# Even mixer of a two-layer trunk: cached sequences in four column groups, their pages fetched ahead, attention of the third pair moved ahead of two recurrences

## The chip, the core and the metric

The kernel runs on one core of a Trainium2 chip. The metric is the device time of one execution in microseconds. Engines: PE is TensorE (PEld its weight loads), DVE is VectorE, ACT is ScalarE, POOL is GpSimd, SP is SyncE, which issues most DMAs.

## What is computed

One inference step of a trunk of two layers for a prompt of 512 tokens and 8 sequences of 4 sample tokens, 544 tokens side by side, in float32. Each layer is a half feed-forward, a mixer, and another half feed-forward. The change lies in layer 0's mixer:

```
def sb_block(q, q_pos, k, v, k_pos, bias):
    z = jnp.einsum('bqhd,bshd->bhqs', q, k, preferred_element_type=jnp.float32) * (SB_HEAD_DIM ** -0.5)
    z = z + bias.astype(jnp.float32)[None, :, None, None]
    mask = k_pos[None, :] < q_pos[:, None]
    log_keep = jnp.where(mask, jax.nn.log_sigmoid(-z), 0.0)
    later = lax.cumsum(log_keep, axis=3, reverse=True) - log_keep
    w = jnp.where(mask, jnp.exp(jax.nn.log_sigmoid(z) + later), 0.0)
    return jnp.einsum('bhqs,bshd->bqhd', w.astype(v.dtype), v)

def sb_lru_mixer(u, past_k, past_v, conv_buf, h0, w_in, ...):
    proj = u @ w_in
    q, k, v, xr, xg = jnp.split(proj, ...)
...
    attn = sb_attention(q, k_all, v_all, q_pos, k_pos, sb_bias).reshape(B, T, SB_WIDTH)
    xc, new_buf = causal_conv(conv_buf, xr, conv_w, conv_b)
    h, h_last = rg_lru(xc, h0, w_a, b_a, w_i, b_i, lam)
    rec = h.astype(u.dtype) * jax.nn.gelu(xg)
    out = jnp.concatenate([attn.astype(u.dtype), rec], axis=-1) @ w_out
```

There are 8 heads of 64, so four pairs of 128 features. Each sample sequence has 256 cached keys and values (past_k, past_v), held as two pages of 128 tokens that a page table picks from a pool of pages in device memory. `rg_lru` is a gated recurrence h = a h + b along the tokens, for 512 features in four tiles of 128.

## The kernel before

The residual x lies on chip as eight tiles of 128 features by 544 tokens; beside it stand xh and xl, the high and low half of the normalised x, each eight tiles. Every linear is three matmuls per tile (`mm3`, L362 to L364): high weights by xh, high weights by xl, low weights by xh, over 256 and 288 columns. Weights are fetched by SP, ACT makes their high half wh (L323) and VectorE their low half wl (L324).

`even_mixer` (L823) walks through a string of tokens, `EVEN_ORDER` (L818):

- Q, V, L, X with a number: linears of one pair's queries and keys, of its values, of a tile of the recurrence and of its output gate.
- A: prompt attention of a pair (`prompt_attention`, L696): eight pieces of 128 to 512 columns, each a chain from PE (z, L707 to L709) over ACT and VectorE (t, mx, sh, sl) back to PE (L720 to L726), to ACT (wt) and to PE again (pv, L729).
- F, G, E, S: gate weights, gates, gelu, and the recurrence of a tile (`lru_scan`, L612, the scan itself on VectorE at L624); T writes the states out; P splits a tile's result into the halves that the output linear reads, which lie in xh[4..7] and xl[4..7].
- K0 and K1: scores of sample sequences 0 to 3 and 4 to 7 against their cached keys (`sample_scores`, L741).
- W: weights from the scores (`sample_weights`, L766). U: weights times cached values (`sample_values`, L787).
- O1 and O0: output linear over the recurrence's and the attention's tiles.

The string sets priorities; a scheduler then interleaves the instructions of each engine, and the resulting order of each engine is fixed when the kernel is built. An engine, and the DMA queue of POOL, runs its own order strictly.

In K, a sequence's two pages are each fetched by an indirect DMA that POOL issues (`page`, L733) into one of six buffers, transposed in four pieces on PE (tp, L751), copied to kt by VectorE or ACT (L753, L755), and multiplied with the queries (sc, L758): 32 stationary columns, that is one group of 32 of the 128 columns of PE, 256 long. In U, wT holds the transposed weights, and each page of values is multiplied with 32 columns of it (po, L805), 512 long; a last matmul adds the sample's own tokens (L806), os and oT (L807, L812) bring the result into feature order, and four splits write it into yh and yl. A page of values is fetched when its matmul's turn comes near.

A matmul of plain float32 runs as two passes, so 32 matmul rows of the scores are 64 records in the trace.

## Time and profile before

| | |
|---|---|
| median of 3 runs | 1924.73 us (1924.58 to 1926.36) |
| profiled execution | 1924.04 us, its span 1922.3 us |
| PE busy | 1872.1 us, 97% |
| weight loads (PEld) busy | 1792.7 us, 93% |
| VectorE busy | 1080.6 us, 56% |
| ACT busy | 836.6 us, 44% |
| POOL busy | 125.5 us, 7% |
| mean granted clock of PE | 0.993 |

The span runs from the first to the last instruction. Busy time of matmuls contains their pipelined tails, so a busy PE is not PE at its peak. The even mixer's second half, in which the change lies, is the stretch from about 470 to 600 us.

### The profile page before, as it was taken

How to read it: one execution, taken by the hardware profiler on the slowest of the kernel's cores; microseconds unless marked ns; L12 is line 12 of the kernel's file. 1: busy time of each engine (PE TensorE's matmuls, PEld its weight loads, DVE VectorE, ACT ScalarE, POOL GpSimd, SP SyncE). 2: the span in 40 equal slices, each digit the busy share in tenths (PEclk: the TensorE clock that was granted, in tenths of full speed). 3: DMA queues.
4: the chain of work that ended last, by engine and by line, in shares of the span. 5: the costliest groups of instructions: out<-in, count | busy, mean ns of one | idle time of the engine just before them, and what ended most of it. 6: DMA issues, size and time to landing. Idle time of an engine off the chain costs nothing.

```text
span 1922.3 us, 36590 instructions
## 1 busy us (share of the span) xinstructions
PE 1872.1 (97%) x15037; PEld 1792.7 (93%) x15037; DVE 1080.6 (56%) x2563; ACT 836.6 (44%) x1733; POOL 125.5 (7%) x237
## 2 busy tenths in 40 slices
PE   7999999999899999999999999899998999999999
PEld 7999999889768999999999999899998998999998
DVE  7444435786756544433544433688978877444422
ACT  6333324777744433322433322475775646333221
POOL 0000002111320000000000000112111100000000
PEclk9999999999999999999999999999999999999999
DMA  4333233322332333323333332333443332233232
GB/s 134 88 89 89 77 88 104 85 56 78 86 103 84 88 88 88 88 79 88 97 88 88 88 93 78 89 88 83 109 125 76 93 91 69 83 86 88 85 112 68
DMA packets 315972, 171.03 MB, mean 89 GB/s; under 512 B 28470, under 2 KB 310278, under 8 KB 315804
## 3 DMA queue, kind: packets, MB, share of 16 engines
q1 hardware_dynamic: 313244, 160.30, 29.7%
q0 software_dynamic: 2560, 8.39, 1.5%
q8 instruction: 118, 1.93, 0.4%
q14 instruction: 50, 0.41, 0.1%
HBM read 158.01 MB, written 10.65 MB: 88 GB/s over the span
## 4 chain that ended last, share of the span: by engine, by line
PE 84%; DVE 7%; ACT 4%; issue 2%; DMA 2%; POOL 1%; SPq 0%; ACTq 0%; DVEq 0%; POOLq 0%
PE lin L362 25%; PE lin L363 24%; PE lin L364 24%; PE pv L729 1%; DVE wl L324 1%; ACT wh L323 1%; PE sc L758 1%; PE po L805 1%; DMA raw<-in_w_ffn_in 1%; DVE acc L1106 1%; DVE LT L1224 1%; DVE ltmp L1223 1%; PE s L1451 0%; ACT f L100 0%; DMA raw<-in_w_in_odd 0%
## 5 line engine op out<-in xcount | busy, mean ns | idle before, releaser
L362 PE MATMUL lin<-xh,wh 128*128 128x256 f32 (+2 forms) x2992 | 873.8, 292 | 19.5 <-DVE sz L1537 4.5
L363 PE MATMUL lin<-xl,wh 128*128 128x256 f32 (+2 forms) x2992 | 871.1, 291 | 1.1 <-DVE xl L371 1.0
L364 PE MATMUL lin<-xh,wl 128*128 128x256 f32 (+2 forms) x2992 | 865.2, 289 | 0.8 <-DVE wl L324 0.8
L362 PEld LDWEIGHTS lin<-xh,wh 128*128 128x128 f32 (+1 forms) x2992 | 564.7, 189 | 26.7 <-ACT wh L323 8.4
L364 PEld LDWEIGHTS lin<-xh,wl 128*128 128x128 f32 (+1 forms) x2992 | 566.3, 189 | 6.1 <-issue 4.1
L363 PEld LDWEIGHTS lin<-xl,wh 128*128 128x128 f32 (+1 forms) x2992 | 564.9, 189 | 5.3 <-issue 1.7
L323 ACT ACTIVATE wh<-raw 128x1024 fp32r<-128x1024 f32 x261 | 275.8, 1057 | 493.3 <-PE lin L363 425.6
L324 DVE TENSOR_TENSOR wl<-raw,wh 128x1024 fp32r<-128x1024 f32 x261 | 317.4, 1216 | 89.5 <-PE lin L364 87.7
L362 PE MATMUL lin<-hh,wh 128*128 128x288 f32 (+1 forms) x1024 | 295.7, 289 | 0.0
L363 PE MATMUL lin<-hl,wh 128*128 128x288 f32 (+1 forms) x1024 | 295.4, 288 | 0.0
L364 PE MATMUL lin<-hh,wl 128*128 128x288 f32 (+1 forms) x1024 | 294.9, 288 | 0.0
L363 PEld LDWEIGHTS lin<-hl,wh 128*128 128x128 f32 x1024 | 193.0, 188 | 0.2
L364 PEld LDWEIGHTS lin<-hh,wl 128*128 128x128 f32 x1024 | 192.7, 188 | 0.1
L362 PEld LDWEIGHTS lin<-hh,wh 128*128 128x128 f32 x1024 | 192.5, 188 | 0.1
L401 DVE TENSOR_TENSOR sg<-lin,rstd 128x256 f32<-128x256 f32 (+1 forms) x128 | 55.9, 438 | 161.3 <-PE lin L364 161.3
L406 DVE TENSOR_TENSOR pr<-lin,rstd 128x256 f32<-128x256 f32 (+1 forms) x128 | 56.5, 441 | 155.3 <-PE lin L364 155.1
L370 ACT ACTIVATE hh<-pr 128x256 fp32r<-128x256 f32 (+1 forms) x128 | 55.1, 431 | 202.4 <-DVE pr L407 202.2
L423 DVE SCALAR_TENSOR_TENSOR x<-lin,x 128x256 f32<-128x256 f32 x64 | 28.2, 441 | 168.7 <-PE lin L364 168.7
L371 DVE TENSOR_TENSOR hl<-pr,hh 128x256 fp32r<-128x256 f32 (+1 forms) x128 | 56.6, 442 | 62.1 <-ACT hh L370 62.0
L100 ACT ACTIVATE sg<-sg 128x256 f32<-128x256 f32 (+1 forms) x128 | 53.7, 422 | 55.9 <-DVE sg L401 55.9
L267 ACT ACTIVATE xh<-x,vec 128x544 fp32r<-128x544 f32 (+2 forms) x64 | 39.6, 632 | 73.1 <-DVE x L423 59.3
L1106 DVE SCALAR_TENSOR_TENSOR acc<-XP,cw,acc 128x568 f32<-128x568 f32 x72 | 58.9, 818 | 2.1 <-ACT acc L1104 1.8
(480 smaller groups left out, 2091.3 us busy)
## 6 DMA issues: line engine op xcount, KB each, us to landing
raw<-in_w_ffn_in SPq DMA_DIRECT2D x128, 512.0 KB
raw<-in_w_ffn_out SPq DMA_DIRECT2D x64, 512.0 KB
raw<-in_w_in_odd SPq DMA_DIRECT2D x32, 512.0 KB
raw<-in_w_in_even SPq DMA_DIRECT2D x20, 512.0 KB
raw<-in_w_out_even SPq DMA_DIRECT2D x8, 512.0 KB
S<-in_state_dn_S SPq DMA_DIRECT2D x8, 512.0 KB
out_dn_S_sample<-S SPq DMA_DIRECT2D x8, 512.0 KB
raw<-in_w_out_odd SPq DMA_DIRECT2D x8, 512.0 KB
```

Source lines behind the costliest of these rows:

```text
L100: i = self.nc.scalar.activation(out, in_, func, **kw).ins
L267: nc.scalar.activation(xh, x, AF.Copy, scale=g)
L323: nc.scalar.activation(self.h, raw, AF.Copy)
L324: nc.vector.tensor_tensor(self.l, raw, self.h.bitcast(F32), op=ALU.subtract)
L362: nc.tensor.matmul(ps[:n], lhsT=wh, rhs=rh, start=(i == 0), stop=False)
L363: nc.tensor.matmul(ps[:n], lhsT=wh, rhs=rl, start=False, stop=False)
L364: nc.tensor.matmul(ps[:n], lhsT=wl, rhs=rh, start=False, stop=(i == len(terms) - 1))
L370: nc.scalar.activation(yh, src, AF.Copy)
L371: nc.vector.tensor_tensor(yl, src, yh.bitcast(F32), op=ALU.subtract)
L401: nc.vector.tensor_tensor(s, ps, E.rstd[:, c0:c0 + cn], op=ALU.mult)
L406: nc.vector.tensor_tensor(p_, ps, E.rstd[:, c0:c0 + cn], op=ALU.mult)
L1106: nc.vector.scalar_tensor_tensor(a, XP[:, j:j + XW - 3], cw[j], a, op0=ALU.mult, op1=ALU.add)
```

## The change

**Scores.** `sample_scores` no longer works sequence by sequence. For each half hf (four sequences), each page i and each head pair p it transposes the four sequences' pieces into one tile, copies it in one operation (ACT for even p, VectorE for odd), and issues four matmuls of 128 columns, one per sequence, each into its own 32 of the 128 columns. The scores tile moves from PSUM tag "s" to tag "pv", which attention's pv shares, and one copy to zs of 128 rows stands in place of four of 32. The first transposes of K0 are tied behind the linear matmul last issued by then.

**Values.** `sample_values` runs over the page i outside and the four sequences inside, in four column groups; after each page index it issues two of O1's eight output tiles.

**Pages.** J1 fetches K1's pages into xh[0..3] and xl[0..3], whose content is used up by then (`SPARE`); Y fetches the value pages of the first half into the XP buffers and the xg tiles and of the second half into xh and xl. O0 takes those tiles again afterwards.

**Recurrence.** In `lru_scan` the memset and the state copy (128x8 each) move from POOL to VectorE.

**Order.** A2 stands ahead of S2 and S3, P0 and P1 ahead of K1, and O1 is no token of its own any more.

What moves is seen in the order of three engines' instructions. First TensorE at one sequence's scores, before (tp is a transpose of a page, sc the scores, lin a linear, z and pv attention, m small transposes):

```order
L751 MATMUL tp_5827<-ident,page_5825 128x128 x3
L721 MATMUL z_5505<-sl_5517,negtri 128x256
L725 MATMUL z_5505<-sh_5496,negones 128x128
L726 MATMUL z_5505<-sl_5497,negones 128x128
L751 MATMUL tp_5827<-ident,page_5825 128x128
L663 MATMUL m_5927<-ident,f_5874 128x128 x2
L362 MATMUL lin_6363<-xh_89,wh_6359 128x256
L758 MATMUL sc_5833<-kt_5816,qb_3639 32x256
L758 MATMUL sc_5833<-kt_5816,qb_4163 32x256
L758 MATMUL sc_5833<-kt_5816,qb_4622 32x256
L758 MATMUL sc_5833<-kt_5816,qb_5752 32x256
L729 MATMUL pv_5392<-wt_5524,vz_3436 128x256
```

and the same place in the changed kernel:

```order
L367 MATMUL lin_6440<-xh_6_90,wh_6394 128x288
L368 MATMUL lin_6440<-xl_14_98,wh_6394 128x288
L772 MATMUL sc_5770<-kt_5779,qb_3639 32x128 x4
L772 MATMUL sc_5770<-kt_5779,qb_4163 32x128 x4
L726 MATMUL z_6109<-sl_6121,negtri 128x128
L369 MATMUL lin_6440<-xh_6_90,wl_6395 128x288
L367 MATMUL lin_6440<-xh_7_91,wh_6394 128x288
L368 MATMUL lin_6440<-xl_15_99,wh_6394 128x288
L369 MATMUL lin_6440<-xh_7_91,wl_6395 128x288
L772 MATMUL sc_5770<-kt_5800,qb_4622 32x128 x4
L763 MATMUL tp_5811<-ident,page_5777 128x128
L763 MATMUL tp_5811<-ident,page_5771 128x128
```

Four matmuls of one sequence in a row have become pieces of four matmuls, one for each of four sequences ("x4"), set among linears.

Second, TensorE at the values (po), before:

```order
L805 MATMUL po_6265<-page_6269,wT_6261 32x512
L720 MATMUL z_6145<-sh_6156,negtri 128x128
L721 MATMUL z_6145<-sl_6157,negtri 128x128
L805 MATMUL po_6265<-page_6272,wT_6261 32x512
L805 MATMUL po_6265<-page_6275,wT_6261 32x512
L805 MATMUL po_6265<-page_6278,wT_6261 32x512
L362 MATMUL lin_6501<-xh_90,wh_6483 128x288
L363 MATMUL lin_6501<-xl_98,wh_6483 128x288
L805 MATMUL po_6265<-page_6281,wT_6261 32x512
L364 MATMUL lin_6501<-xh_90,wl_6484 128x288
```

and now, where page names that begin with xh or xl lie in the tiles of x:

```order
L734 MATMUL pv_6108<-wt_6264,vz_3437 128x384
L817 MATMUL po_6321<-page_6072,wT_6317 32x512
L817 MATMUL po_6321<-page_6066,wT_6317 32x512
L817 MATMUL po_6321<-page_6068,wT_6317 32x512
L817 MATMUL po_6321<-page_6070,wT_6317 32x512
L817 MATMUL po_6321<-page_6080,wT_6317 32x512
L817 MATMUL po_6321<-page_6074,wT_6317 32x512
L817 MATMUL po_6321<-page_6076,wT_6317 32x512
L817 MATMUL po_6321<-page_6078,wT_6317 32x512
L821 MATMUL po_6321<-vs,wT_6317 128x512
L807 MATMUL m_6456<-ident,zs 128x128 x2
L725 MATMUL z_6267<-sh_6278,negtri 128x512
```

The eight matmuls of a half stand in one piece, with no linear between them, and the own-token matmul follows at once.

Third, the queue of POOL between the copies of the queries (qa) for the last two attentions, before:

```order
L693 COPY qa_3432<-qa_3432 64x512
L736 DMA page_5945<-in_cache_k,idx 128x512
L736 DMA page_5953<-in_cache_k,idx 128x512
L736 DMA page_5968<-in_cache_k,idx 128x512
L845 COPY ks<-kn_5580 128x32
L736 DMA page_5976<-in_cache_k,idx 128x512
L693 COPY qa_3433<-qa_3433 64x512
L736 DMA page_5991<-in_cache_k,idx 128x512
```

and now, ahead of the second of these copies:

```order
L744 DMA xh_807_5956<-in_cache_k,idx 128x512
L744 DMA xl_811_5964<-in_cache_k,idx 128x512
L744 DMA page_6074<-in_cache_v,idx 128x512
L744 DMA page_6076<-in_cache_v,idx 128x512
L744 DMA page_6078<-in_cache_v,idx 128x512
L744 DMA page_6080<-in_cache_v,idx 128x512
L698 COPY qa_3433<-qa_3433 64x512
L744 DMA page_5825<-in_cache_k,idx 128x512
L744 DMA page_5827<-in_cache_k,idx 128x512
L744 DMA page_6066<-in_cache_v,idx 128x512
```

Four pages of values now stand ahead of the copy for A3, and the last two pages of K0 (page_5825, page_5827) behind it.

The diff, without the first hunk's unchanged surroundings:

```diff
@@ -138,10 +138,15 @@
         nc.vector.memset(E.kv[:, j:j + 1], v)
     E.eps, E.one, E.tiny = E.kv[:, 0:1], E.kv[:, 1:2], E.kv[:, 2:3]
     E.x = [E.rp.tile([P, NT], F32, name=f"x{k}") for k in range(KD)]
-    E.xh = [E.rp.tile([P, NT], F32R, name=f"xh{k}") for k in range(KD)]
-    E.xl = [E.rp.tile([P, NT], F32R, name=f"xl{k}") for k in range(KD)]
+    E.xh = [split_tile(E, f"xh{k}") for k in range(KD)]
+    E.xl = [split_tile(E, f"xl{k}") for k in range(KD)]
     E.xsq = E.rp.tile([P, NT], F32, name="xsq")
     E.rstd = E.rp.tile([P, NT], F32, name="rstd")
+
+
+def split_tile(E, tag, dt=F32R):
+
+    return E.rp.tile([P, NT], dt, tag=tag, name=E.nm(tag), bufs=1)
 
 
 VROWS = [("norm_ffn1", 16), ("norm_mix", 16), ("norm_ffn2", 16), ("lru_conv_w", 16), ("lru_conv_b", 4),
@@ -361,7 +366,7 @@
             rh, rl = xh[k][:, c0:c0 + cn], xl[k][:, c0:c0 + cn]
             nc.tensor.matmul(ps[:n], lhsT=wh, rhs=rh, start=(i == 0), stop=False)
             nc.tensor.matmul(ps[:n], lhsT=wh, rhs=rl, start=False, stop=False)
-            nc.tensor.matmul(ps[:n], lhsT=wl, rhs=rh, start=False, stop=(i == len(terms) - 1))
+            E.last_mm = nc.tensor.matmul(ps[:n], lhsT=wl, rhs=rh, start=False, stop=(i == len(terms) - 1)).ins
         evac(h, c0, cn, ps)
 
 
@@ -618,8 +623,8 @@
     E.act(th, th, AF.Ln, bias=E.tiny)
     E.act(th, th, AF.Exp, scale=0.5)
     nc.vector.tensor_tensor(ig, ig, th, op=ALU.mult)
-    nc.gpsimd.memset(seg(a)[:, :, 0:1], 0.0)
-    nc.gpsimd.tensor_copy(seg(ig)[:, :, 0:1], E.lst[:, t, 24:].unsqueeze(2))
+    nc.vector.memset(seg(a)[:, :, 0:1], 0.0)
+    nc.vector.tensor_copy(seg(ig)[:, :, 0:1], E.lst[:, t, 24:].unsqueeze(2))
     h = r
     nc.vector.tensor_tensor_scan(h, a, ig, 0.0, op0=ALU.mult, op1=ALU.add)
     nc.gpsimd.tensor_copy(E.lso[:, t, 27:28], h[:, T - 1:T])
@@ -730,33 +735,42 @@
     split_to(E, yh[p][:, :T], yl[p][:, :T], pv)
 
 
-def page(E, ap, name, o):
-
-    t = ap.tile([P, NE], F32, tag="XP", name=E.nm("page"), bufs=PB)[:, :512]
-    E.nc.gpsimd.indirect_dma_start(out=t, out_offset=None, in_=E.I[name].rearrange("a n s h d -> (a n s) (h d)"),
+def page(E, ap, name, o, home="XP"):
+
+    if home[0] == "x" and home[1] in "hl":
+        t = split_tile(E, home, F32)
+    else:
+        t = ap.tile([P, NE if home == "XP" else NT], F32, tag=home, name=E.nm("page"), bufs=PB if home == "XP" else 4)
+    E.nc.gpsimd.indirect_dma_start(out=t[:, :512], out_offset=None, in_=E.I[name].rearrange("a n s h d -> (a n s) (h d)"),
                                    in_offset=bass.IndirectOffsetOnAxis(ap=E.idx[:, o:o + 1], axis=0))
-    return t
-
-
-def sample_scores(E, ap, qb, ks, zs, hf):
-
-    nc = E.nc
-    for b in range(4 * hf, 4 * hf + 4):
-        rows = slice(32 * (b % 4), 32 * (b % 4) + 32)
-        kt = ap.tile([P, 4, 256], F32, tag="kt", name=E.nm("kt"))
-        for i in range(2):
-            kp = page(E, ap, "cache_k", 2 * b + 1 - i)
+    return t[:, :512]
+
+
+def pages(E, ap, name, hf, i, homes):
+    return [page(E, ap, name, 2 * (4 * hf + b) + 1 - i, homes[b]) for b in range(4)]
+
+
+def sample_scores(E, ap, qb, ks, zs, hf, kps):
+
+    nc = E.nc
+    sc = E.pm.tile([P, 512], F32, tag="pv", name=E.nm("sc"))[:, :256]
+    for i in range(2):
+        kp = kps[i]()
+        for p in range(4):
+            if p % 2 == 0:
+                kt = ap.tile([P, 2, 4, P], F32, tag="kt", name=E.nm("kt"))
             tp = E.pm.tile([P, 4, P], F32, tag="s", name=E.nm("tp"))
-            for p in range(4):
-                nc.tensor.transpose(tp[:, p], kp[:, p * P:(p + 1) * P], E.ident)
-            if i:
-                nc.vector.tensor_copy(kt[:, :, P:], tp)
+            tr = [nc.tensor.transpose(tp[:, b], kp[b][:, p * P:(p + 1) * P], E.ident).ins for b in (3, 0, 1, 2)]
+            for a, b in zip(tr, ([E.last_mm] if hf == 0 else tr[:1]) + tr):
+                if a is not b:
+                    E.after(a, b)
+            if p % 2:
+                nc.vector.tensor_copy(kt[:, 1], tp)
             else:
-                nc.scalar.activation(kt[:, :, :P], tp, AF.Copy)
-        ps = E.pm.tile([P, 256], F32, tag="s", name=E.nm("sc"))
-        for p in range(4):
-            nc.tensor.matmul(ps[rows], lhsT=qb[p][:, b], rhs=kt[:, p], start=(p == 0), stop=(p == 3))
-        nc.vector.tensor_copy(zs[rows, hf, :256], ps[rows])
+                nc.scalar.activation(kt[:, 0], tp, AF.Copy)
+            for b in range(4):
+                nc.tensor.matmul(sc[32 * b:32 * b + 32, i * P:(i + 1) * P], lhsT=qb[p][:, 4 * hf + b], rhs=kt[:, p % 2, b], start=(p == 0), stop=(p == 3), skip_group_check=True)
+    nc.vector.tensor_copy(zs[:, hf, :256], sc)
     ps = E.pm.tile([P, NS], F32, tag="s", name=E.nm("sn"))
     for p in range(4):
         nc.tensor.matmul(ps, lhsT=qb[p][:, 4 * hf:4 * hf + 4].rearrange("p a b -> p (a b)"), rhs=ks[:, p], start=(p == 0), stop=(p == 3))
@@ -784,7 +798,7 @@
     E.act(zs, zs, AF.Exp, bias=E.sbs)
 
 
-def sample_values(E, ap, zs, vs, yh, yl):
+def sample_values(E, ap, zs, vs, yh, yl, vps, between):
     nc = E.nc
     os = ap.tile([P, 2, 512], F32, tag="kt", name=E.nm("os"))
     for hf in range(2):
@@ -798,12 +812,13 @@
         nc.gpsimd.memset(wT[NS:64, 2], 0.0)
         nc.scalar.activation(wT[:NS, 2], wps2, AF.Copy)
         po = E.pm.tile([P, 512], F32, tag="s", name=E.nm("po"))
-        for g in range(4):
-            b = 4 * hf + g
-            for i in range(2):
-                vp = page(E, ap, "cache_v", 2 * b + 1 - i)
-                nc.tensor.matmul(po[32 * g:32 * g + 32], lhsT=wT[:, i, 32 * g:32 * g + 32], rhs=vp, start=(i == 0), stop=False)
-        nc.tensor.matmul(po, lhsT=wT[:64, 2], rhs=vs[:64], start=False, stop=True)
+        for i in range(2):
+            vp = vps[2 * hf + i]
+            mm = [nc.tensor.matmul(po[32 * g:32 * g + 32], lhsT=wT[:, i, 32 * g:32 * g + 32], rhs=vp[g], start=(i == 0), stop=False, skip_group_check=True).ins for g in (3, 0, 1, 2)]
+            for a, b in zip(mm, [E.last_mm] + mm):
+                E.after(a, b)
+            between(2 * hf + i)
+        nc.tensor.matmul(po, lhsT=wT[:64, 2], rhs=vs[:64], start=False, stop=True, skip_group_check=True)
         nc.vector.tensor_copy(os[:, hf], po)
     oT = E.pm.tile([P, 4, NS], F32, tag="s", name=E.nm("oT"))
     for hf in range(2):
@@ -815,9 +830,10 @@
 
 
 PB = 6
-EVEN_ORDER = "Q0 L0 V0 A0 Q1 V1 A1 Q2 X0 L1 F L2 G0 G1 G2 L3 X1 X2 G3 X3 E S0 S1 S2 V2 S3 A2 Q3 K0 V3 P2 P3 K1 A3 W U P0 P1 O1 T O0"
+EVEN_ORDER = "Q0 L0 V0 A0 Q1 V1 A1 Q2 X0 L1 F L2 G0 G1 G2 L3 X1 X2 G3 X3 E S0 S1 V2 A2 S2 S3 Q3 K0 V3 J1 P2 P3 P0 P1 K1 Y A3 W U T O0"
 TB = 8
 ZB = 2
+SPARE = [[f"x{c}{k}" for k in range(4)] for c in "hl"]
 
 
 def even_mixer(E, w_in, w_out, nxt):
@@ -864,10 +880,13 @@
             def attend(p):
                 prompt_attention(E, ap, p, *Q[p], yh, yl)
 
-            def out(part):
-                ws = wide(E, w_out, list(range(4 * part, 4 * part + 4)))
-                for m in range(KD):
-                    w = ws(m)
+            wide_out = {}
+
+            def out(part, ms=range(KD)):
+                if part not in wide_out:
+                    wide_out[part] = wide(E, w_out, list(range(4 * part, 4 * part + 4)))
+                for m in ms:
+                    w = wide_out[part](m)
 
                     def ev(h, c0, cn, ps):
                         xx = E.x[m][:, c0:c0 + cn]
@@ -877,7 +896,7 @@
                     if part == 0 and nxt is not None:
                         split_x(E, m, *nxt)
 
-            L, X, gate, env = {}, {}, {}, {}
+            L, X, gate, kp = {}, {}, {}, {}
             for tok in EVEN_ORDER.split():
                 c, i = tok[0], int(tok[1]) if tok[1:] else 0
                 if c == "Q":
@@ -909,12 +928,21 @@
                 elif c == "K":
                     if i == 0:
                         zs = ap.tile([P, 2, 288], F32, name="zs")
-                    sample_scores(E, ap, qb, ks, zs, i)
+                    if i not in kp:
+                        kp[i] = [lambda j=j: pages(E, ap, "cache_k", i, j, ("XP",) * 4) for j in range(2)]
+                    sample_scores(E, ap, qb, ks, zs, i, kp[i])
+                elif c == "J":
+                    kp[i] = [lambda v=pages(E, ap, "cache_k", i, j, SPARE[j]): v for j in range(2)]
+                elif c == "Y":
+                    vp = [pages(E, ap, "cache_v", j // 2, j % 2, hm) for j, hm in enumerate([("XP",) * 4, ("xg",) * 4] + SPARE)]
                 elif c == "W":
                     sample_weights(E, ap, zs)
                 elif c == "U":
-                    sample_values(E, ap, zs, vs, yh, yl)
+                    sample_values(E, ap, zs, vs, yh, yl, vp, lambda n: out(1, range(2 * n, 2 * n + 2)))
                 elif c == "O":
+                    if i == 0:
+                        for k in range(4):
+                            E.xh[k], E.xl[k] = split_tile(E, f"xh{k}"), split_tile(E, f"xl{k}")
                     out(i)
 
 
```

## Rows read from the trace of the kernel before

**Rows 1.** The page: busy time by engine, and the chain that ended last.

```profile
PE 1872.1 (97%) x15037; PEld 1792.7 (93%) x15037; DVE 1080.6 (56%) x2563; ACT 836.6 (44%) x1733; POOL 125.5 (7%) x237
...
PE 84%; DVE 7%; ACT 4%; issue 2%; DMA 2%; POOL 1%; SPq 0%; ACTq 0%; DVEq 0%; POOLq 0%
```

**Rows 2.** Windows of 20 us: length, busy us (instructions) by engine, granted clock, DMA.

```profile
480.00:500.00 20.00, 16.95 (x108) 14.97 (x106) 18.00 (x36) 15.89 (x32) 5.26 (x11) 0.91 0.36 103
...
560.00:580.00 20.00, 19.87 (x84) 9.66 (x82) 7.63 (x16) 7.42 (x18) 8.54 (x10) 1.00 0.43 128
580.00:600.00 20.00, 20.00 (x133) 13.40 (x133) 7.62 (x17) 6.57 (x13) 2.07 (x3) 1.00 0.22 70
600.00:620.00 20.00, 19.50 (x157) 19.27 (x156) 15.62 (x27) 10.20 (x15) 0.00 (x0) 1.00 0.28 84
```

**Rows 3.** Timeline of PE at 478 to 483 us: start, duration, operation, idle before it.

```profile
478.77 1.48 PE L758 MATMUL sc<-kt,qb 128*32 128x256 f32 x6
482.95 0.55 PE L362 MATMUL lin<-xh,wh 128*128 128x256 f32 x1 [2.70 <-DVE f L646]
```

**Rows 4.** Windows of 2 us behind that idle time, columns as in rows 2.

```profile
482.00:484.00 2.00, 1.05 (x5) 1.08 (x6) 2.00 (x5) 1.85 (x4) 1.11 (x2) 0.69 0.23 57
484.00:486.00 2.00, 2.00 (x12) 2.00 (x11) 1.84 (x6) 0.98 (x3) 1.83 (x4) 0.50 0.28 39
```

**Rows 5.** Timeline of PE: one sequence's scores.

```profile
508.49 1.91 PE L758 MATMUL sc<-kt,qb 128*32 128x256 f32 x8
```

**Rows 6.** Groups of the scores and of the values: ns min/median/max, first and last start.

```profile
L758 PE MATMUL sc<-kt,qb x64: 379/379/403, 478.8 to 548.8; 128*32 128x256 f32 x64
L805 PE MATMUL po<-page,wT x32: 592/592/617, 563.3 to 588.0; 128*32 128x512 f32 x32
```

**Rows 7.** Timeline of PE: two visits of the values.

```profile
566.98 1.90 PE L805 MATMUL po<-page,wT 128*32 128x512 f32 x6
...
577.92 1.90 PE L805 MATMUL po<-page,wT 128*32 128x512 f32 x4
```

**Rows 8.** Odd mixer, narrow passes in groups: timeline of PE, and the group.

```profile
1328.90 1.51 PE L1451 MATMUL s<-S,wqz 128*32 128x128 f32 x46
...
L1451 PE MATMUL s<-S,wqz x256: 272/273/297, 1297.5 to 1567.4; 128*32 128x128 f32 x128
```

**Rows 9.** Timeline of PE and of VectorE around 322 us.

```profile
322.43 0.66 PE L751 MATMUL tp<-ident,page 128*128 128x128 f32 x4 [1.68 <-DMA page<-in_cache_k,idx]
324.05 0.30 PE L751 MATMUL tp<-ident,page 128*128 128x128 f32 x1 [0.96 <-DMA page<-in_cache_k,idx]
...
322.27 1.22 DVE L324 TENSOR_TENSOR wl<-raw,wh 128x1024 fp32r<-128x1024 f32 x1
```

**Rows 10.** Timeline of PE and of VectorE from the last scores to O0.

```profile
549.88 0.97 PE L762 MATMUL sn<-ks,qb 128*128 128x32 f32 x8
...
559.05 0.44 PE L793 MATMUL m<-ident,zs 128*128 128x128 f32 x2
...
588.56 1.12 PE L806 MATMUL po<-vs,wT 64*128 64x512 f32 x2
...
591.02 1.11 PE L812 MATMUL oT<-sel,os 128*64 128x16 f32 x32
...
596.41 0.28 PE L362 MATMUL lin<-xh,wh 128*128 128x256 f32 x1
596.53 0.28 PE L363 MATMUL lin<-xl,wh 128*128 128x256 f32 x1
...
599.78 0.36 PE L362 MATMUL lin<-yh,wh 128*128 128x256 f32 x1
...
594.90 0.19 DVE L371 TENSOR_TENSOR yl<-oT,yh 128x32 fp32r<-128x32 f32 x1 [0.26 <-ACT yh L370]
```

**Rows 11.** POOL: a page issue in the timeline, and groups of page issues with idle time.

```profile
474.42 1.97 POOL L736 DMA_INDIRECT page<-in_cache_k,idx  x1
...
L736 POOL DMA_INDIRECT page<-in_cache_v,idx x16 | 15.1, 945 | 34.0 <-PE po L805 21.2 <-PE tp L751 5.6 <-PE z L721 3.6
```


## The prediction

> **What bounds the kernel now.** I read the profile's page first, then windows of 20 us over the even mixer's second half, then the waits of TensorE there, then single visits in the timeline. The page says that TensorE (PE) is busy 97% of the span and carries 84% of the chain that ended last [rows 1]: time falls where TensorE loses instructions or idle time, and hardly elsewhere. The profiled execution took 1924.04 us, of which 1922.3 are span; it stands 0.7 us under the median of 1924.73, so a sum made in its trace is carried to the median by adding 0.7.
>
> In the windows [rows 2] TensorE is busy but poorly used from 480 to 600 us. In 560 to 580 it issues 84 groups with weight loads busy only 9.66 us of 20, where 600 to 620, with linears almost alone, has 19.27. "Busy" hides this: a pass with 32 stationary columns counts as busy like one with 128. So the reader should look at what the passes do. The one large idle time is 2.70 us before a linear at 482.95, ended by VectorE [rows 3], with the granted clock at 0.69 and then 0.50 just behind it, that is falling from the 2.4 to the 1.2 GHz level after this idle time [rows 4].
>
> **The scores and values, the main term.** A visit for the scores is 8 passes of 256 columns in one 32-column group: 1.91 us [rows 5], of which the last pass's own duration is 379 ns [rows 6], so (1.91 − 0.38)/7 = 0.219 us per pass. 64 passes make 14.0 us. The values are 32 passes of 512 columns, 592 ns each [rows 6] but begun sooner one after the other; the visit of four gives (1.90 − 0.59)/3 = 0.436 us per pass. A visit of six takes the same 1.90 us [rows 7]: its two pairs for different sequences already ran side by side. There are two such visits, so 28 slots, 12.2 us. Together 26.2 us.
>
> The change issues the same multiplications with four sequences in four column groups: each "x4" in its order is one head pair for four sequences, 128 columns long. The trace has the like of it: in the odd mixer 46 passes of 128 columns in groups of 32 take 1.51 us, the last one's own 273 ns among it [rows 8], so (1.51 − 0.27)/45 = 0.0275 us each. The scores become 128 such passes, 3.5 us; the values 32 passes of four times the length at 0.110, another 3.5 us. Saved: 26.2 − 7.0 = 19.2 us. The three score calls (1.3 us) that ran in the idle place just before 482.95 [rows 3] were covered by VectorE's lateness, so taking them out there buys nothing: **−17.9 us**.
>
> *TensorE: Matmul & The Clock Gate* of the Trainium skill (Part 3, measured speedup) has three column tiles of 32 at 512 columns 2.38 times as fast as one after the other, not 3. By that the 26.2 us would shrink by 3.2 times and the gain be 1.2 us smaller; the row of 46 passes shows the full factor of four, and the sum goes by it.
>
> Changing between linears and narrow passes costs something at each visit; I count 20 visits before and 18 after: nothing.
>
> **Early transposes.** Before, K0's first two pages are transposed far ahead of their use, and TensorE waits 1.68 and 0.96 us for their DMAs [rows 9]. The change pins the first transposes behind a later linear, which removes both. But the low halves of the next weights are written by VectorE from 322.27 to 323.49 [rows 9], and the third linear needs them, so of the time to 324.1 I book **−0.7 us** (bounds 0 and −2.6).
>
> **The VectorE stall at 482.95.** A2 now stands ahead of S2 and S3, so one would think that its first pieces meet fewer recurrences. But the linear at 482.95 was released by VectorE's copy-out f (L646), and from the first scan to that copy-out VectorE's new order still has two scans, their products and the pieces of A2, with four small operations more (memset and state copy, which came from POOL). Booked at **0**; bounds +1, and −4.3 if the 2.70 us and the 1.6 us of lost clock (2 x 0.31 + 2 x 0.50) go [rows 3, 4].
>
> **The tail W, U, O0.** Before, from the last scores at 549.88 to the last split at 594.90 [rows 10] most is linear work of O1. The change spends many of these linears under K0 and K1: in its order only 37 linears lie between the last score and the point from which O0's follow without another operation, and the values stand in one piece of eight and one of two and six, where eleven visits had other work between them. By rows the serial chain there is 9.2 us (sn at 549.88 to m at 559.05), 1 for wT, twice 2.9 for values with their own-token pair (1.12 for the latter), 0.7 for os and 4 from oT to the last split [rows 10]: 21 us, some 25 with VectorE's other work between. TensorE has about 19 us of passes in it (37 linears at 0.12 [rows 10], the attention, the values) and some visits. Cost **+2 us** (bounds 0 and +6).
>
> **Pages on POOL, and the new orders.** POOL's queue is in order. Four value pages, which wait for the P splits to free their buffers, now stand ahead of A3's copy and of K0's last two pages. An issue costs 0.95 us, or 1.97 beside a recurrence on VectorE [rows 11]. Eleven first transposes now wait for others of TensorE, under 0.2 us each. A3's value products wait until K1's scores leave the shared bank. Together **+1 us** (bounds 0 and +3).
>
> Sum: −17.9 − 0.7 + 0 + 2 + 1 = −15.6; 1924.7 − 15.6 = **1909.1 us** (the profiled execution some 1908.4).
>
> **Rivals.**
> (a) The values' gain is lost in the tail. O0 needs yh of every pair, and the chain of 21 to 25 us sets the end, whatever the passes cost. Then 12.2 − 3.5 = 8.7 us come back: 1917.8 us. For it: few linears left there. Against it: VectorE and ACT, which run that chain, are far from full at 580 to 600 (7.62 and 6.57 of 20 us [rows 2]), and its copies get fewer: two zs copies of 128 rows in place of eight of 32. *TensorEngine Tiling (Array Packing)* of the Trainium skill (PSUM Bottleneck) warns that behind a fourfold speedup the copies out of PSUM may bind, which would be this rival; no row here shows them late.
> (b) The stall at 482.95 goes after all: −4.3 more, 1904.8 us, and with no tail cost 1902. For it: that is where the order changed, and the scan that waited for POOL's copy behind a page issue need not any more. Against it: VectorE is busy 18.0 of 20 us there [rows 2].
> (c) Slower: POOL's queue. Twelve issues (eight K, four V pages) stand between the two q copies where four stood. At 1.97 us each [rows 11] that is 23.6 us, and if none of it lies beside other work A3 and K0 come that much later: 1909.1 + 23.6 = 1932.7 us. It decides once TensorE idles over 15.6 us for it; against it, V3 and O1 have 240 linears, at 0.12 us 29 us, to fill the time, and before, POOL's page issues waited for TensorE (21.2 of their 34.0 us [rows 11]), not the reverse.
> (d) The column groups don't overlap for these shapes: no main term, 1924.7 − 0.7 + 3 = 1927.0 us. The row of 46 passes speaks against it.
>
> **The numbers.** Chances: forecast 0.59, (a) 0.15, (b) 0.18, (c) 0.04, (d) 0.04. A measurement of this kernel tells 0.2%, 3.8 us, from no change. Forecast, (a) and (b) are all faster by more: 0.92; (d) is the same: 0.04; (c) slower: 0.04. The range 1902 to 1918.5 takes in (b), most of (a) and the forecast with its bounds.
>
> **What would show it.** Right: scores at about 0.22 us per 8 passes, O0's linears from about 584 instead of 599.78 us [rows 10], nothing changed behind. Wrong in the main term: score passes at 0.11 each. Wrong in the sizes: an idle TensorE over 5 us after K1 (rival a), for pages (c), or none at 482 (b).

## The result and the profile after

The changed kernel takes 1913.92 us (median of 6 runs, 1911.62 to 1920.33), the kernel before 1924.65 us (6 runs). The ratio is 0.9943, with a 95% interval of 0.9932 to 0.9955: 11 us less. The forecast was 1909.1 us in a range of 1902 to 1918.5; the median lies 4.8 us above it. The profiled execution, at 1916.94 us, is one of the longer runs; why, is shown below.

The page of the changed kernel, busy time by engine, answers to [rows 1]:

```profile
PE 1861.2 (97%) x15101; PEld 1793.0 (94%) x15101; DVE 1078.1 (56%) x2565; ACT 836.9 (44%) x1733; POOL 121.2 (6%) x229
```

TensorE has lost 11 us of busy time, and has 64 more records: the scores' 64 passes of 256 columns have become 128 of 128. How they run is seen in the groups and in the timeline of TensorE, which answer to [rows 5 to 8]:

```profile
L772 PE MATMUL sc<-kt,qb x128: 272/285/423, 529.3 to 564.1; 128*32 128x128 f32 x128
```

```profile
549.64 0.28 PE L367 MATMUL lin<-xh,wh 128*128 128x256 f32 x1
550.01 0.42 PE L772 MATMUL sc<-kt,qb 128*32 128x128 f32 x8
550.37 0.66 PE L763 MATMUL tp<-ident,xh 128*128 128x128 f32 x4
...
575.89 1.92 PE L817 MATMUL po<-page,wT 128*32 128x512 f32 x16
577.75 1.12 PE L821 MATMUL po<-vs,wT 64*128 64x512 f32 x2
```

Eight passes of the scores take 0.42 us, of which the last one's own 0.27: 0.02 us each, below the 0.0275 of the forecast. But from the first pass of the eight to the next instruction it is 0.36 us (550.01 to 550.37), where the forecast's sign was 0.22. Sixteen passes of the values take the time of four before (1.92 against 1.90 us [rows 7]).

To see where the time went, I put the start of the k-th linear matmul of one trace beside that of the other. Their number (12528) is the same in both, and so is their order but for a few between the 3265th and the 3482nd, none of them in this table:

```
linear      before     after    difference
 2100        288.0     289.5      +1.5
 2400        330.7     330.2      -0.5
 3000        453.7     455.0      +1.3
 3900        657.0     646.0     -11.0
 8400       1234.5    1223.4     -11.0
 9600       1479.2    1472.2      -7.0
12527       1916.9    1909.8      -7.1
```

The first 1.5 us come in at the start of the program. At the early transposes 2.0 us are gained, in the stretch of the change 12.3 us. In between and far behind, in the odd mixer, 1.8 and 4 us are lost. The windows of the changed kernel show the clock there, third from the right:

```profile
360.00:420.00 60.00, 57.62 (x385) 50.70 (x383) 46.68 (x93) 45.02 (x102) 6.14 (x10) 0.97 0.22 60
1380.00:1440.00 60.00, 58.81 (x604) 54.97 (x603) 45.24 (x171) 40.58 (x123) 8.03 (x18) 0.94 0.42 109
```

and in the second trace of the same kernel (r_after, below):

```profile
360.00:420.00 60.00, 57.78 (x384) 50.79 (x384) 46.91 (x93) 45.30 (x102) 6.14 (x10) 0.97 0.22 61
1380.00:1440.00 60.00, 57.99 (x619) 53.99 (x618) 48.57 (x181) 42.84 (x126) 8.78 (x20) 1.00 0.42 109
```

Before, both windows have 1.00; 60 us at 0.97 and at 0.94 lose 1.8 and 3.6 us. The second loss does not come back in r_after: it is chance of this execution, and makes up for its 3.0 us above the median. The first does come back, and it is not all clock. In the twelve traces of this study in which K0's first transposes are tied, 0.8 to 0.9 us are lost from linear 2400 to 3000 at full clock (six traces), and 1.6 to 1.9 us with this window at 0.97 (the other six); in b_order, which has no tie, nothing. At 379 us TensorE waits 1.97 us for VectorE's copy-out f in the tied kernels, 1.63 us before. So the tie gives back a part of what it gains.

What else was lost stands in TensorE's waits from 440 to 605 us (name, source, us in total, times, longest):

```profile
PE tp L763 <- DMA page<-in_cache_k,idx: 3.2, 1, 3.2
PE z L725 <- ACT sh L375: 2.1, 3, 1.4
PE pv L734 <- ACT wt L100: 1.7, 2, 1.5
PE z L726 <- DVE sl L376: 1.0, 2, 0.8
```

The first line is new; the third is too, 1.5 us of it at one visit at 520.30 us (0.7 us in r_after). Timeline of TensorE and of POOL, and windows of 2 us:

```profile
538.53 0.63 PE L763 MATMUL tp<-ident,page 128*128 128x128 f32 x4 [3.23 <-DMA page<-in_cache_k,idx]
```

```profile
521.86 0.61 POOL L698 CAST qa<-qa 64x512 fp32r<-64x512 f32 x1 [3.50 <-DMA page<-in_cache_v,idx]
532.14 0.96 POOL L744 DMA_INDIRECT page<-in_cache_k,idx  x1 [9.68 <-PE tp L763]
533.41 1.66 POOL L744 DMA_INDIRECT page<-in_cache_k,idx  x1 [0.31 <-issue]
```

```profile
536.00:538.00 2.00, 0.00 (x0) 0.00 (x0) 0.00 (x0) 0.00 (x0) 1.27 (x2) 1.00 1.10 404
538.00:540.00 2.00, 1.27 (x12) 1.08 (x16) 0.00 (x0) 0.81 (x2) 0.00 (x0) 0.87 0.57 209
540.00:542.00 2.00, 2.00 (x14) 1.30 (x10) 0.41 (x1) 1.76 (x4) 0.00 (x0) 0.50 0.00 0
542.00:544.00 2.00, 2.00 (x18) 1.44 (x18) 1.36 (x3) 0.00 (x0) 0.00 (x0) 0.77 0.00 0
```

K0's last two pages are issued at 532.14 and 533.41, after POOL has waited 9.68 us for a transpose, that is for one of the six page buffers to come free. They land beside other fetches at 404 GB/s. TensorE stands still for 3.23 us, and the clock falls to half, the 1.2 GHz level, behind it: 0.87, 0.50 and 0.77 in three windows of 2 us, which loses 1.7 us.

The place of the old stall and the tail, in the timeline of TensorE, answer to [rows 3] and [rows 10]:

```profile
481.36 0.33 PE L725 MATMUL z<-sh,negtri 128*128 128x128 f32 x1 [1.44 <-ACT sh L375]
482.52 0.33 PE L726 MATMUL z<-sl,negtri 128*128 128x128 f32 x1 [0.83 <-DVE sl L376]
483.00 0.39 PE L367 MATMUL lin<-xh,wh 128*128 128x256 f32 x1 [0.15 <-DVE f L651]
...
564.26 1.08 PE L776 MATMUL sn<-ks,qb 128*128 128x32 f32 x8
...
588.71 0.52 PE L367 MATMUL lin<-yh,wh 128*128 128x288 f32 x2 [0.30 <-ACT yh L375]
```

The stall's idle time is 2.42 us (1.44, 0.83 and 0.15) where it was 2.70. From the last scores to O0 it takes 24.4 us, and O0 begins at 588.71 us, where the forecast had about 584.

### The profile page after: what moved, and what is told of

The parts are those of the page before. It is cut to its first block, busy times and chain, and to the rows that moved or that the text cites. A ratio compares the mean times of both kernels' runs of the same rounds, so it can differ in the third digit from the quotient of the medians.

```text
span 1915.2 us, 36694 instructions
## 1 busy us (share of the span) xinstructions
PE 1861.2 (97%) x15101; PEld 1793.0 (94%) x15101; DVE 1078.1 (56%) x2565; ACT 836.9 (44%) x1733; POOL 121.2 (6%) x229
## 4 chain that ended last, share of the span: by engine, by line
PE 58%; DVE 5%; ACT 2%; issue 1%; DMA 1%; POOL 0%; SPq 0%; ACTq 0%; DVEq 0%; POOLq 0%
PE lin L367 18%; PE lin L368 17%; PE lin L369 17%; DVE acc L1134 1%; DVE wl L329 1%; DVE LT L1252 1%; DVE ltmp L1251 1%; PE s L1479 0%; DMA raw<-in_w_in_odd 0%; PE m L1211 0%; DMA raw<-in_w_ffn_in 0%; ACT wh L328 0%; DVE Dn L1165 0%; PE c L1349 0%; DMA grs<-gdr 0%
## 5 line engine op out<-in xcount | busy, mean ns | idle before, releaser
L369 PE MATMUL lin<-xh,wl 128*128 128x256 f32 (+2 forms) x2992 | 865.8, 290 | 0.5 <-DVE wl L329 0.5
L369 PEld LDWEIGHTS lin<-xh,wl 128*128 128x128 f32 (+1 forms) x2992 | 566.8, 189 | 2.6 <-issue 0.8
L369 PE MATMUL lin<-hh,wl 128*128 128x288 f32 (+1 forms) x1024 | 294.9, 288 | 0.0
L369 PEld LDWEIGHTS lin<-hh,wl 128*128 128x128 f32 x1024 | 192.7, 188 | 0.1
```

What stands on the lines that cost most here:

```text
L369: E.last_mm = nc.tensor.matmul(ps[:n], lhsT=wl, rhs=rh, start=False, stop=(i == len(terms) - 1)).ins
```

## The experiments

The experiments ran in groups, and the kernel before was timed beside each group. Differences below are between medians of one group where both kernels ran in it, and else by way of the ratio to the kernel before; where the two ways differ, both are given. The scheduler fixes each engine's order anew for every edit, so some of TensorE's order moves with it: for example in e_pages and e_sc1 behind 532 us, in b_tie from 322 us on. The early fetch (J1, Y) and O1's new places were not run by themselves.

**The changed kernel again (r_after).** No edit.

> The changed kernel once more, so that the other three are read against it on the same chip. Both theories expect about 1914 us with a wide scatter (1911 to 1920), and in the trace again a TensorE wait of some 3 us for K0's last two pages near 535 us. If the scatter is the granted clock alone, span less (1 - mean clock) x span is the same in every run within 1 us.

1913.39 us (6 runs, 1910.18 to 1914.66), ratio 0.9928 (0.9910 to 0.9945), 12.1 us below the kernel before (13.9 by the ratio). The page wait is there again, 3.2 us. Mean clock times span gives 1896.5 us in the median and 1911.2 us for the kernel before: 14.7 us apart. So the changed kernel gives back some 3 us in clock: it loses 15.3 us that way in the median run, the kernel before 11.5 us (17 runs). The scatter is not the clock alone, though: the products spread over 6.6 us, not 1, and the clock's three digits account for at most 2 of that.

**K0's last pages elsewhere (e_pages).**

```diff
+    elif home[:3] == "gwl":
+        if home == "gwl0":
+            E.gwp = E.yp.tile([P, 2, 4 * P], F32, tag="gwl", name=E.nm("gwp"), bufs=1)
+        t = E.gwp[:, int(home[3])]
...
-kp[i] = [lambda j=j: pages(E, ap, "cache_k", i, j, ("XP",) * 4) for j in range(2)]
+kp[i] = [lambda j=j: pages(E, ap, "cache_k", i, j, (("XP",) * 4, ("XP", "XP", "gwl0", "gwl1"))[j]) for j in range(2)]
```

> K0's last two pages go into the tile of the gate weights' low halves, dead by then, and no longer wait for two XP buffers. Theory 1 (what the forecast lacks is this page wait, 3.2 us, and the 1.7 us of clock that it costs): 4 to 5 us below the changed kernel, about 1909.5 us, and no idle time at K0's second page in the trace. Theory 2 (the pages are only what happens to come last; V3, the P splits or the transposes' own waits would end there anyway): within 1 us of the changed kernel.

1907.53 us (5 runs), 5.9 us below the changed kernel beside it (4.2 by the ratios) and 17.9 below the kernel before; ratio 0.9906 (0.9886 to 0.9926). The line on pages is gone from TensorE's waits, and the windows at the same place are full, at full clock:

```profile
536.00:538.00 2.00, 2.00 (x22) 1.36 (x20) 1.33 (x3) 1.37 (x4) 0.44 (x1) 1.00 1.00 362
538.00:540.00 2.00, 2.00 (x22) 1.60 (x21) 1.48 (x3) 0.52 (x1) 0.20 (x1) 1.00 0.15 53
540.00:542.00 2.00, 2.00 (x18) 2.00 (x18) 0.30 (x2) 0.35 (x1) 0.00 (x0) 1.00 0.00 0
```

The time lost in clock falls to 11.4 us in the median run, that of the kernel before (13.4 when the same kernel ran again as p_ref). Theory 1 holds, and the wait cost more than its own length: 3.2 us idle and 1.7 in clock make 4.9. What is left of the 5.9 is not shown; other waits of TensorE shrink too, that of pv from 1.7 to 0.2 us.

**Scores in one column group (e_sc1).** Each head pair's sums stand alone in its own rows; the sum over the pairs is left out.

```diff
-nc.tensor.matmul(sc[32 * b:32 * b + 32, ...], ..., start=(p == 0), stop=(p == 3), ...)
+nc.tensor.matmul(sc[32 * p:32 * p + 32, ...], ..., start=(b == 0), stop=(b == 3), ...)
```

> Scores: the four matmuls of a head pair are all put into one column group (the group of the pair's number), so they run one after the other; the sums over the pairs are left out, so the scores are not the reference's. Theory 1 (TensorE binds there, the passes side by side are the gain): 128 passes at 0.107 instead of 0.0275 us, +10.2 us against the changed kernel. Theory 2 (K's chain over ACT and VectorE binds, the scores were hidden anyway): +3 us or less.

1921.07 us, ratio 0.9978 (0.9965 to 0.9991), 7.7 above the changed kernel (9.6 by the ratios). In its timeline of TensorE the visit of eight passes took

```profile
529.54 1.06 PE L772 MATMUL sc<-kt,qb 128*32 128x128 f32 x8
```

1.06 in place of 0.42 us; 16 times eight passes make 10.2 us. Three quarters of that or more arrive at the end, so theory 1 holds: TensorE binds. In this trace K0's page wait is 2.5 us instead of 3.2.

**Values, page behind page (e_po1).**

```diff
-        for i in range(2):
-            vp = vps[2 * hf + i]
-            mm = [... for g in (3, 0, 1, 2)]
+        order = [(g, i) for g in (3, 0, 1, 2) for i in range(2)]
+        mm = [... for g, i in order]
...
```

> Values: the same matmuls, but a sequence's two pages one behind the other, so that only neighbouring sequences overlap: five slots of two passes where two were, for each half, 2 x 3 x 0.87 = 5.2 us more on TensorE. Theory 1 (TensorE binds in the tail as well): +4 to +5.5 us against the changed kernel. Theory 2 (the chain over W, U and the splits sets the tail's end, rival a of the prediction): +1.5 us or less.

1913.20 us, ratio 0.9933 (0.9915 to 0.9950), no change, but the experiment did not do what it was meant to, as its timeline of TensorE shows:

```profile
574.10 1.94 PE L816 MATMUL po<-page,wT 128*32 128x512 f32 x16
```

Sixteen passes in 1.94 us as against 1.92: the groups ran side by side in the order of page behind page too. So it says nothing about the tail; it says that the values run side by side once the eight matmuls stand in one piece with their pages there, and that their order among themselves did not matter here.

**Values in one column group (e_po1b).** The own-token matmul goes first, and all sequences of a half are summed into one group's rows.

```diff
+nc.tensor.matmul(po, lhsT=wT[:64, 2], rhs=vs[:64], start=True, stop=False, ...)
...
-mm = [nc.tensor.matmul(po[32 * g:32 * g + 32], ...) for g in (3, 0, 1, 2)]
+mm = [nc.tensor.matmul(po[:32], ..., start=False, ...) for g in (3, 0, 1, 2)]
...
```

> Values again, this time all eight matmuls of a half in one column group (with the own-token matmul first), because in the last attempt the second page's matmuls ran beside other groups anyway and little work was added. Left out: the values of the four sequences of a half are summed into one group's rows, so sample outputs are not the reference's. 32 passes at 0.436 us instead of 8 slots: 10.5 us more on TensorE. Theory 1 (TensorE binds in the tail as well): +8 to +10.5 us against the changed kernel, about 1923. Theory 2 (the chain over W, U and the splits sets the tail's end, and the values' passes lie beside it): +4 us or less.

1926.33 us, ratio 0.9997 (0.9988 to 1.0007), against 0.9928: some 13 us more than the changed kernel. In its timeline eight passes now take 3.62 us:

```profile
586.42 3.62 PE L818 MATMUL po<-page,wT 128*32 128x512 f32 x8
```

That is above theory 1's band and far from theory 2's, so rival (a) of the prediction falls: in the tail TensorE binds. That it is more than the 10.5 us added fits the clock, which loses 17.3 us in the median run here against 15.3 in r_after; what lowered it is not shown.

**The tie alone, in the kernel before (b_tie).**

```diff
...
+                if b == 0:
+                    E.after(t, E.last_mm)
```

> The kernel before, with K0's first transposes tied behind the last linear matmul issued ahead of them, nothing else. Theory 1 (the two early page waits cost what the linears behind them came late, 2.1 us by the start of the next linears in the two traces): 1.8 to 2.3 us below the kernel before. Theory 2 (the prediction's: VectorE's low halves hold the linears to 323.5 us, so 0.7 us; or the wait turns up again at K0): 0 to 0.8 us below it.

1924.09 us, ratio 0.9989 (0.9979 to 1.0000): 2.1 us less, 2.7 by the medians. That is near theory 1, but the interval reaches from 0 to 4 us and takes in theory 2, so the times do not decide. The early page waits are gone (1.3 us for VectorE's f stands in their place), but the stall has grown, in the timeline of TensorE:

```profile
485.48 0.36 PE L362 MATMUL lin<-xh,wh 128*128 128x256 f32 x1 [4.13 <-DVE f L646]
```

It is 4.13 us where it was 2.70 [rows 3]: K0's early scores had stood in front of it, as six passes of 1.48 us [rows 3], and now come later.

**The order alone, in the kernel before (b_order).** S2 and S3 behind A2, memset and state copy on VectorE.

```diff
...
-E S0 S1 S2 V2 S3 A2 Q3
+E S0 S1 V2 A2 S2 S3 Q3
```

> The kernel before, with A2 ahead of S2 and S3 and the scans' memset and state copy on VectorE, nothing else. Theory 1 (the prediction's: VectorE has as much ahead of the linear that waits at 483 us as before): within 1 us of the kernel before. Theory 2 (rival b: the stall and its clock loss go): 3 to 4.3 us below it.

1920.82 us, ratio 0.9974 (0.9964 to 0.9985): 5.0 us less, 6.0 by the medians. Theory 1, mine, falls; theory 2's 3 to 4.3 us lie within the interval (2.9 to 6.9). With the scores as cover the stall is nearly gone from the timeline of TensorE:

```profile
482.42 1.48 PE L758 MATMUL sc<-kt,qb 128*32 128x256 f32 x6
483.95 0.33 PE L720 MATMUL z<-sh,negtri 128*128 128x128 f32 x1
485.11 0.33 PE L721 MATMUL z<-sl,negtri 128*128 128x128 f32 x1 [0.83 <-DVE sl L371]
485.59 0.39 PE L362 MATMUL lin<-xh,wh 128*128 128x256 f32 x1 [0.15 <-DVE f L646]
```

**The order undone, in e_pages (p_order), beside e_pages again (p_ref).** The order string's piece as in the line with the minus above.

> e_pages once more, as the base of the other two on the same chip. 1907 to 1908.5 us, 17 to 18 us below the kernel before; mean granted clock about 0.994 in most runs, as in the kernel before.

> e_pages with S2 and S3 ahead of A2 again, the order of the kernel before; nothing else. Theory 1 (the order is worth in the changed kernel what it is worth alone, since early scores no longer cover the stall at 480 us; in b_tie TensorE idles 4.1 us there): 3 to 5 us above e_pages. Theory 2 (the prediction's: the order is worth nothing): within 1 us of it.

p_ref 1908.22 us, ratio 0.9911 (0.9892 to 0.9931); p_order 1914.18 us, ratio 0.9937 (0.9917 to 0.9957), 6.0 above it (5.0 by the ratios). Its timeline and its window:

```profile
486.08 0.47 PE L725 MATMUL z<-sh,negtri 128*128 128x128 f32 x1 [5.80 <-ACT sh L375]
```

```profile
480.00:490.00 10.00, 3.96 (x17) 3.12 (x16) 10.00 (x23) 4.73 (x11) 4.30 (x9) 0.61 0.34 93
```

Without the scores in front and with four recurrences ahead, TensorE idles 5.80 us, and the clock is at 0.61 of full speed over 10 us. So theory 1 holds: the order is worth 5 to 6 us in e_pages.

**Three tries to shorten what is left of the stall**, all in e_pages: A2 ahead of S1 too (p_s0), products of two recurrences on POOL (p_mul), Q3 ahead of S2 and S3 (p_q3).

```diff
-E S0 S1 V2 A2 S2 S3 Q3 K0
+E S0 V2 A2 S1 S2 S3 Q3 K0
```

> e_pages with A2 ahead of S1 too (E S0 V2 A2 S1 S2 S3). Theory 1 (TensorE's 2.3 us at 480 us wait for VectorE behind the second recurrence): some 2 us below e_pages, about 1905.5 us. Theory 2 (the gates of the later tiles hold the work buffers that A2 needs, so A2's chain starves): above e_pages by 1 us or more.

```diff
-    nc.vector.tensor_tensor(g[:, :T], h[:, :T], g[:, :T], op=ALU.mult)
+    (nc.gpsimd if t < 2 else nc.vector).tensor_tensor(g[:, :T], h[:, :T], g[:, :T], op=ALU.mult)
```

> e_pages with the products of the first two recurrences with their gates (128x512) on POOL instead of VectorE. Theory 1 (TensorE's 2.3 us at 480 us are VectorE's queue): 1 to 2 us below e_pages. Theory 2 (POOL's page issues and copies stand behind the products, and slow VectorE beside them): the same or above.

```diff
-E S0 S1 V2 A2 S2 S3 Q3 K0
+E S0 S1 V2 A2 Q3 S2 S3 K0
```

> e_pages with the last pair's linears ahead of S2 and S3 as well (S0 S1 V2 A2 Q3 S2 S3), so that VectorE's order has nothing of S2 and S3 ahead of the copy-out for which TensorE waits at 483 us. Theory 1 (that queue is the rest of the stall): the 2.3 us of idle time shrink to under 0.5, some 2 us below e_pages, about 1906 us. Theory 2 (S2 and S3 hold the buffers of K0's and the values' pages, and POOL's queue makes K0 wait again): a page wait comes back in the trace, 2 us or more above e_pages.

p_s0 1910.28 us, ratio 0.9924 (0.9911 to 0.9938): not below e_pages (0.9906), from which the intervals do not tell it apart, so neither theory is shown. p_mul 1910.57 us, ratio 0.9923 (0.9902 to 0.9944), 2.4 above p_ref, which its interval takes in; TensorE's longest wait for VectorE grew to 4.2 us, which speaks against theory 1. p_q3 1921.55 us, ratio 0.9973 (0.9959 to 0.9988), some 12 us above p_ref. There the stall is gone (0.51 us left), but the next window of its 20 us windows is poorly filled:

```profile
500.00:520.00 20.00, 12.57 (x62) 10.32 (x61) 17.42 (x35) 15.08 (x31) 13.54 (x17) 0.84 0.70 200
```

TensorE is busy 12.57 of 20 us, VectorE 17.42. Theory 1 was right on the stall and wrong on the time; theory 2 had the sign but not the mechanism, for of TensorE's waits there none is for a page: 2.3 us are for ACT, 0.5 for VectorE, and the longest, 2.9, has no source in the profile. The clock loses 19.2 us in the median run, against 13.4 in p_ref. That the recurrences' work was only put off to where attention needs VectorE fits this, but is not shown.

The best kernel of the study is e_pages, 1907.53 us and, as p_ref, 1908.22 us.

## Why the prediction was right or wrong

The forecast was 15.6 us less; the two medians are 10.7 and 12.1 less, inside the range. The main mechanism held; what lacks is mainly the step on pages, and two of the other terms came out by chance or through a wrong reading.

**The passes side by side (−17.9 us): right in the mechanism, and in size by two errors that cancel.** Adding up, over the rows of TensorE in the stretch of the linears 3000 to 3900, the time from each row's start to the next row's, the scores fall from 17.6 us (2.9 of them the stall behind the sixth pass) to 5.8, the values from 13.3 to 4.7: 17.5 us. The like of it in the prediction is 19.2, before the 1.3 were taken off. Nearly all of the 1.7 that lack are in the scores: eight passes cost 0.36 us with the change to and from other work, not 0.22, so the visits that I put at nothing were not free. The 1.3 that I took off were not lost, because the new order shortened the wait that these scores had covered (see the stall below). The two experiments that put the passes into one group cost 7.7 and 13 us. For the values the trace agrees with the row of 46 passes [rows 8], not with the factor of 2.38 for three tiles that the Trainium skill's *TensorE: Matmul & The Clock Gate* (Part 3, Measured speedup vs the span model) has: 16 passes in 1.92 us against 4 in 1.90 is a factor of four. For the short visits of the scores it is less, 1.06 against 0.42 us.

**The early transposes (−0.7): misread.** The linears came 2.0 us earlier, and 0.8 of it was lost again by linear 3000. I had the third linear wait for the low halves wl of [rows 9]. In the changed kernel that operation runs where it ran (1.5 us later, like the whole program there), and the third linear (L369) begins before it is done, so it is not the one that this linear needs. What holds the first linear is VectorE's f. The timelines of VectorE and of TensorE:

```profile
323.73 1.22 DVE L329 TENSOR_TENSOR wl<-raw,wh 128x1024 fp32r<-128x1024 f32 x1
...
323.51 0.39 PE L367 MATMUL lin<-xh,wh 128*128 128x256 f32 x1 [1.29 <-DVE f L651]
...
323.85 0.28 PE L369 MATMUL lin<-xh,wl 128*128 128x256 f32 x1
```

So 1.29 us of waiting stand where 2.64 stood.

**The stall (0): right by chance.** Its idle time went from 2.70 to 2.42 us, but as the sum of two effects that I had not seen: the order of S2 and S3 behind A2 is worth 5 to 6 us (b_order, p_order), and tying K0's transposes takes away the scores that covered the wait (4.13 us in b_tie, 5.80 in p_order). My reason, that VectorE's queue stays as long, was read from the number of operations ahead of the copy-out f; in the changed kernel TensorE waits only 0.15 us for f, and 2.27 for the sh and sl of attention.

**The tail (+2): too dear.** The chain's length was right (24.4 us against 21 to 25), but TensorE has hardly any idle time in it (0.5 us before z, 0.3 before O0), and e_po1b shows that TensorE binds there.

**Pages and orders (+1, at most 3): this step failed.** It cost 5.9 us by the medians of e_pages, 4.9 by the trace. I looked at POOL's queue, where four value pages had moved ahead of K0's last two, and priced issues. What held them was the ring of six buffers: the two pages wait for the first page's transposes on TensorE itself, so their issue, 4.1 us to landing (the median of the two in the list of DMA issues) and the clock behind the gap stand in series with TensorE. My bound left the clock out altogether.

With what was measured the sum is −17.5 − 2.0 + 0.8 − 0.3 + 0.8 + 5.9 = −12.3 us, against 10.7 and 12.1 us less in the two medians. It mixes rows of single traces with medians. The 0.2 to 1.6 us that are left are not assigned; the clock behind 379 us, some 0.8 to 1.0 us in both traces of the changed kernel, is one candidate.

Of the rivals, (b) named the right place, and b_order shows its gain in the kernel before, but with the tie the wait there stayed; by its own terms its lower time is 1902.8 us, not 1902. (c) named the right queue, but not the ring of buffers that held it, and the cost was a quarter of what it had.

## What to carry to other kernels

When operands are fetched ahead, count the buffers of the ring against the operands that one step needs at once: eight pages through six buffers put a whole fetch in series with the engine that frees them. An idle gap on TensorE is to be priced with the clock that may fall behind it, here 1.7 us behind 3.2. Before calling a wait unchanged, look at what stands in front of it and whether the change takes that away.

## What the hardware did that I had not expected

In e_po1 the four sequences' matmuls stood in TensorE's queue two by two, each pair in one column group, and yet the passes began in fours: four between 574.10 and 574.14 us, the next four from 574.55, all 16 in 1.94 us. By the queue's order one group after the other would have been two or three at a time. The timeline of the weight loads has the same fours, two of them at first:

```profile
574.10 0.18 PEld L816 LDWEIGHTS po<-page,wT 128*32 128x32 f32 x8 [0.55 <-issue]
574.55 0.15 PEld L816 LDWEIGHTS po<-page,wT 128*32 128x32 f32 x4 [0.28 <-issue]
574.98 0.15 PEld L816 LDWEIGHTS po<-page,wT 128*32 128x32 f32 x4 [0.28 <-issue]
```

The records do not name the group, but a load's record names the semaphore that it waits for, which tells most of the matmuls apart. In the queue the eight matmuls wait for semaphores 100, 112, 115, 117, 116, none, 117 and 111. The load for 115, the third, starts at 574.109 us and that for 116, the fifth, at 574.122; the load for 112, the second, which goes to the same column group as the first, starts only at 574.552. So a matmul was overtaken by matmuls of other groups, and TensorE does not start everything strictly in its own order, as I had said of the engines. *TensorE: Matmul & The Clock Gate* of the Trainium skill (Part 3, The mechanism) has matmuls start and end strictly in the order of the program; these starts read otherwise.

The clock does not fall behind every gap: at nearly the same idle time of 2.3 to 2.4 us near 480 us the windows from 480 to 500 show 1.00 in the first trace of the changed kernel and 0.83 in the second (r_after):

```profile
480.00:500.00 20.00, 17.33 (x119) 15.02 (x119) 19.83 (x43) 16.27 (x35) 5.76 (x11) 1.00 0.26 84
480.00:500.00 20.00, 17.66 (x102) 15.72 (x103) 18.14 (x41) 14.18 (x31) 4.72 (x10) 0.83 0.23 72
```
